# Seven products for eight in half of the Fourier columns of an in-projection, with the Fourier work and the rotation put behind them

## The chip, the cores and the metric

The kernel runs on one core of a Trainium2 chip. The metric is device time in microseconds (us), the median of the runs; lower is better. All arithmetic is in 32-bit floats. To keep float precision, the kernel writes each operand of a matrix product as a high part (`h`, the value rounded to the format that TensorE takes) and a low part (`l`, what the rounding left), and forms high·high + low·high + high·low: three matmuls where one would do.

## The reference, cut to what matters

```python
def hybrid_layer(x, ln_mix_g, w_in, w_fourier, attn_sink, ...):
    h = rmsnorm(x, ln_mix_g)
    z = h @ w_in                      # 2048 -> 2560 columns: 1024 Fourier, 1024 q, 256 k, 256 v
    zf, q, k, v = ...                 # split by columns
    of = fourier_mix(zf, w_fourier)   # 8 groups of 128 channels: Re(2-D DFT), then a 128x128 map
    q, k = apply_rope(q, cos, sin), apply_rope(k, cos, sin)
    oa = window_attention(q, k, v, attn_sink)
    mixed = concatenate([rmsnorm(of, g_of), rmsnorm(oa, g_oa)], axis=-1)
    x = x + mixed @ w_out
    u = relu(rmsnorm(x, ln_mlp_g) @ w_up)
    return x + (u * u) @ w_down
```

It is applied to 512 tokens of a prompt and 256 tokens of a sample, 768 in all (`T`). `HALF` is 384 tokens.

## The kernel before, in words

The kernel has five stages: a prologue (norm of x, transposes to `hh`, `hl`, and the v columns), the in-projection for all other columns, attention together with the output projection, the up-projection and the down-projection. The up-projection already uses seven products for eight. The change touches the in-projection alone, with the work that is laid beside it.

**The in-projection** takes the columns in units of 256: four units of the Fourier group, one of k, four of q (`cols`). A unit is four pieces, one for each quarter of the depth of 2048. A piece is one load of 512 KB (`piece_load`, tile `raw`), one split of the weights into `wh` and `wl` (ScalarE copies, VectorE subtracts), and 48 matmuls: two blocks of 128 columns, four depth blocks of 128, the three products of high and low parts, two halves of the tokens. After the fourth piece VectorE takes the four PSUM banks `pz` off as `zs`, scaled by `rb`, and a DMA writes them to DRAM (`zf`, `zk`, `zq`). There are 36 pieces, numbered from 0, and then attention.

**Other work is hung on pieces** by the table `todo`. `after(p, fn)` puts a function behind piece `p` or, for half numbers, in the middle of the next piece. Its matmuls then stand at this place in TensorE's own order, which is written out by hand. The other engines' orders are made by a scheduler, with the order of the code as priority. Only in the last four pieces are ScalarE and VectorE also in the order of the code. A DMA is issued by SyncE (loads), ScalarE (most stores) or GpSimd (a few stores); each of these issues in order, so a load that has to wait holds up every load behind it.

Three kinds of work hang there. First the eight Fourier groups (`load_group`, `fold`, `stage1`, `stage2`), one group for each two pieces, from piece 4.5 to piece 21.5. Then `fourier_norm` and `open_attention`, which loads the rotary tables. Then 16 rotation jobs, from piece 23 to 34.5: four `keys` and twelve `queries`. Each job loads half of the tokens of 128 rows back from DRAM into `rx`, and the rows with halves exchanged into `ry` by four small loads; GpSimd multiplies `ry` by the sines, VectorE multiplies `rx` by the cosines and adds; a query job then splits the result into a high tile `rh` and a low tile `rl` and stores both (`qh`, `ql`). `rx` and `ry` have two buffers each, `rh` and `rl` one. At piece 34.5 `load_of` loads the Fourier output of the first 128 tokens in two halves, `ofr`, into `ry` buffers; the output projection needs it as attention begins.

Of the kernel before, what the change touches and what calls it, by code (L numbers as in the profile page):

```python
# [20 lines left out]
P = 128  # L21
# [19 lines left out]
def hybrid_encoder(ctx: ExitStack, tc: tile.TileContext, a: dict):  # L41
# [3 lines left out]
    def f32(ap):  # L45
        return ap.bitcast(F32)
# [67 lines left out]

    zf_d = [dpool.tile([P, T], F32, tag=f"zf{i}", name=f"zf{i}") for i in range(FG)]
# [79 lines left out]
    with ExitStack() as ph:  # L195
# [142 lines left out]
        fp = fctx.enter_context(tc.tile_pool(name="fp", bufs=1, reuse_waits="tile"))  # L338
        cc = fp.tile([P, 2, P], F32, tag="cc", name="cc")
        nc.sync.dma_start(cc[:], a["c_chan"])  # L340
        tabh = fp.tile([P, 4, 256], F32R, tag="tabh", name="tabh")
        tabl = fp.tile([P, 4, 256], F32R, tag="tabl", name="tabl")
        for i in range(2):
            tab = fp.tile([P, 2, 256], F32, tag="zf", name="tab", bufs=2)
            nc.sync.dma_start(tab[:], a["c_pos"][:, 2 * i : 2 * i + 2, :])
            split(tabh[:, 2 * i : 2 * i + 2, :], tabl[:, 2 * i : 2 * i + 2, :], tab[:])
        ssf = fp.tile([P, T], F32, tag="ssf", name="ssf")
# [92 lines left out]
        kt = {}  # L440

        def open_attention():
            kp = kt["kp"] = kctx.enter_context(tc.tile_pool(name="kp", bufs=1, side="right", reuse_waits="tile"))
            for name, shape, src in (
                ("mask", [P, 384], a["c_mask"]), ("cosr", [P, T], a["c_cos"]), ("sinr", [P, T], a["c_sin"]),
# [3 lines left out]
                nc.sync.dma_start(kt[name][:, : src.shape[1]], src)  # L449
            kt["kdh"] = kp.tile([P, NKV, T], F32R, tag="kdh", name="kdh")  # L450
# [12 lines left out]
        def rows2(src, s):  # L463

            t0 = slice(s * HALF, (s + 1) * HALF)
            x, y = (kt["kp"].tile([P, 1, 512], F32, tag=c, name=c, bufs=n)[:, :, :HALF] for c, n in (("rx", 2), ("ry", 2)))
# [6 lines left out]
            return x[:, 0, :], t0  # L473

        def keys(i, s):
            x, t0 = rows2(zk_d[i], s)
# [21 lines left out]
        def load_q(u):  # L498
# [9 lines left out]
            y = kt["kp"].tile([P, 4, P], F32, tag="ry", name="ry", bufs=2)  # L508
# [21 lines left out]
        todo = {}  # L530

# [3 lines left out]
        for g in range(FG):  # L535
            p0 = 5.5 + 2 * g
# [1052 lines left out]
```

## Time and profile before

| | us |
|---|---|
| median of 3 runs (lowest, highest) | 2610.72 (2610.60, 2612.91) |
| the profiled execution, its span | 2610.32, 2608.5 |
| prologue, until the first matmul of the in-projection that runs on without a break | 0 to 56.7 |
| in-projection with the work beside it | 56.7 to 396.8 |
| attention and output projection | 396.8 to 752.4 |
| up-projection | 752.4 to 1686.2 |
| down-projection and the end | 1686.2 to 2608.5 |

The profile is of one execution. PE is TensorE, PEld its weight loads, DVE VectorE, ACT ScalarE, POOL GpSimd, SP SyncE; a "q" behind an engine's name is the DMA issuing of that engine. A group row gives line, engine, operation, tiles, shape and count, then busy us and mean ns of one, then the idle time before and what ended it. A chain row gives start, duration and what ran. A DMA row gives the size of one transfer and its median us from issue to landing.

### The profile page before, as it was taken

How to read it: one execution, taken by the hardware profiler on the slowest of the kernel's cores; microseconds unless marked ns; L12 is line 12 of the kernel's file. 1: busy time of each engine (PE TensorE's matmuls, PEld its weight loads, DVE VectorE, ACT ScalarE, POOL GpSimd, SP SyncE). 2: the span in 40 equal slices, each digit the busy share in tenths (PEclk: the TensorE clock that was granted, in tenths of full speed). 3: DMA queues.
4: the chain of work that ended last, by engine and by line, in shares of the span. 5: the costliest groups of instructions: out<-in, count | busy, mean ns of one | idle time of the engine just before them, and what ended most of it. 6: DMA issues, size and time to landing. Idle time of an engine off the chain costs nothing.

```text
span 2608.5 us, 35166 instructions
## 1 busy us (share of the span) xinstructions
PE 2595.5 (100%) x13692; PEld 2378.2 (91%) x13692; DVE 1739.1 (67%) x2186; ACT 1075.8 (41%) x1543; POOL 246.7 (9%) x347
## 2 busy tenths in 40 slices
PE   9999999999999999999999999999999999999998
PEld 9999998888899999999999999988888888888887
DVE  6334448777655656555777787757776765777687
ACT  6233327775323333333454445433333333333335
POOL 1011212234210011000000000010000000000000
PEclk9999999999999999999999999999999999999999
DMA  5323466345674555466666666685543672554364
GB/s 183 117 94 111 134 217 190 114 126 169 199 228 150 173 171 172 148 205 242 206 215 214 221 232 217 216 325 178 182 158 111 210 248 74 177 186 157 97 208 157
DMA packets 255047, 465.17 MB, mean 178 GB/s; under 512 B 20080, under 2 KB 151712, under 8 KB 254240
## 3 DMA queue, kind: packets, MB, share of 16 engines
q1 hardware_dynamic: 189936, 305.01, 36.5%
q10 hardware_dynamic: 53120, 110.46, 11.1%
q0 software_dynamic: 11824, 47.46, 5.4%
q8 instruction: 107, 1.75, 0.3%
q14 instruction: 60, 0.49, 0.1%
HBM read 344.10 MB, written 118.75 MB: 177 GB/s over the span
## 4 chain that ended last, share of the span: by engine, by line
PE 98%; DVE 1%; DMA 1%; issue 0%; ACT 0%; POOL 0%; SPq 0%; DVEq 0%; POOLq 0%; ACTq 0%
PE pu L970 36%; PE pd L1405 35%; PE pz L592 11%; PE pm L824 9%; PE pv L235 1%; PE s L635 1%; PE t L692 1%; PE o L711 1%; PE pa L396 1%; PE pe L417 0%; PE ptx L134 0%; PE pt L134 0%; DMA raw<-in_w_in 0%; DVE wl L70 0%; PE pz L417 0%
## 5 line engine op out<-in xcount | busy, mean ns | idle before, releaser
L970 PE MATMUL pu<-xf,wh 128*128 128x384 f32 x3072 | 781.1, 335 | 0.0
L970 PEld LDWEIGHTS pu<-xf,wh 128*128 128x128 f32 x3072 | 554.2, 188 | 1.5 <-ACT o L988 1.3
L1405 PE MATMUL pd<-wl,sh 128*128 128x512 f32 x1332 | 518.5, 389 | 0.0
L1405 PE MATMUL pd<-wh,sh 128*128 128x512 f32 x1332 | 518.5, 389 | 0.0
L1405 PE MATMUL pd<-wh,sl 128*128 128x512 f32 x1332 | 518.3, 389 | 0.0
L970 PE MATMUL pu<-xf,wl 128*128 128x384 f32 x1536 | 514.0, 335 | 0.0
L1382 ACT ACTIVATE wh<-rd 128x1024 fp32r<-128x1024 f32 x200 | 202.3, 1054 | 522.3 <-PE pd L1405 425.0
L1392 DVE TENSOR_TENSOR wl<-rd,wh 128x1024 fp32r<-128x1024 f32 x200 | 236.1, 1222 | 226.2 <-ACT wh L1382 225.5
L950 ACT ACTIVATE wh<-ur 128x1024 fp32r<-128x1024 f32 x160 | 170.0, 1063 | 382.0 <-PE pu L970 210.0
L1405 PEld LDWEIGHTS pd<-wh,sh 128*128 128x128 f32 x1332 | 250.2, 188 | 51.7
L1405 PEld LDWEIGHTS pd<-wl,sh 128*128 128x128 f32 x1332 | 250.2, 188 | 51.7
L1405 PEld LDWEIGHTS pd<-wh,sl 128*128 128x128 f32 x1332 | 250.1, 188 | 51.7 <-DVE sl L1393 0.3
L970 PEld LDWEIGHTS pu<-xf,wl 128*128 128x128 f32 x1536 | 288.4, 188 | 0.0
L956 DVE TENSOR_TENSOR wl<-ur,wh 128x1024 fp32r<-128x1024 f32 x160 | 195.6, 1222 | 75.4 <-ACT wh L950 75.4
L991 DVE TENSOR_TENSOR o<-pu,o 128x768 f32<-128x768 f32 x160 | 153.0, 956 | 122.4 <-PE pu L970 114.9
L592 PE MATMUL pz<-hh,wh 128*128 128x384 f32 x576 | 147.3, 336 | 0.0
L592 PE MATMUL pz<-hh,wl 128*128 128x384 f32 x576 | 146.5, 335 | 0.0
L592 PE MATMUL pz<-hl,wh 128*128 128x384 f32 x576 | 146.3, 335 | 0.0
L1375 DVE TENSOR_TENSOR rd<-rd 128x1024 f32<-128x1024 f32 x112 | 131.8, 1219 | 0.0
L970 PE MATMUL pu<-xs,wh 128*128 128x384 f32 x512 | 130.0, 335 | 0.0
L950 ACT ACTIVATE wh<-sx 128x1024 fp32r<-128x1024 f32 x64 | 67.8, 1062 | 131.0 <-PE pu L970 102.8
L70 DVE TENSOR_TENSOR wl<-raw,wh 128x1024 fp32r<-128x1024 f32 x56 | 68.3, 1225 | 68.9 <-ACT wh L69 68.8
(247 smaller groups left out, 3723.4 us busy)
## 6 DMA issues: line engine op xcount, KB each, us to landing
rd<-in_w_down SPq DMA_DIRECT2D x176, 512.0 KB, 4.8
ur<-in_w_up SPq DMA_DIRECT2D x128, 512.0 KB, 3.9
sr<-sd SPq DMA_DIRECT2D x95, 384.0 KB, 5.0
pd<-o ACTq DMA_DIRECT2D x60, 384.0 KB, 2.3
o<-pd POOLq DMA_DIRECT2D x60, 384.0 KB, 5.9
sd<-sm ACTq DMA_DIRECT2D x60, 384.0 KB, 2.7
raw<-in_w_in SPq DMA_DIRECT2D x40, 512.0 KB, 3.5
raw<-in_w_out SPq DMA_DIRECT2D x32, 512.0 KB, 4.3
```

The costliest lines, as they stand in the source:

```text
L70: nc.vector.tensor_tensor(out=lo, in0=src, in1=f32(hi), op=ALU.subtract)
L235: nc.tensor.matmul(pv[:, :256], l[j][:, i, t0], wv[j][r][:, i, :], start=(n == 0 and i == 0), stop=(n == 11 and i == 3),)
L592: nc.tensor.matmul(ps[c][s][:, :HALF], w[:, i, cs], h[j][:, i, s * HALF : (s + 1) * HALF], start=first and n == 0, stop=stop and n == 2,)
L824: nc.tensor.matmul(ps, l(k), w[:, k % 2, :], start=(k == 0 and n == 0), stop=(k == 7 and n == 2))
L950: nc.scalar.activation(wh[:], raw[:], AF.Copy)
L956: nc.vector.tensor_tensor(out=wl[:], in0=raw[:], in1=f32(wh[:]), op=ALU.subtract)
L970: nc.tensor.matmul(ps[:, t, :HALF], w[:, i, t * P : (t + 1) * P], xb[:, o, i, :], start=(s == first_of[bank] and i == 0 and n == 0), stop= ...
L991: nc.vector.tensor_tensor(out=o, in0=src, in1=o, op=ALU.add)
L1375: add = lambda x, y, op: nc.vector.tensor_tensor(out=x[:], in0=x[:], in1=y[:], op=op)
L1382: nc.scalar.activation(wh[:], t[:], AF.Copy)
L1392: nc.vector.tensor_tensor(out=wl[:], in0=t[:], in1=f32(wh[:]), op=ALU.subtract)
L1405: nc.tensor.matmul(o, l[:, q, ts], w[:, ns], start=(j == j0 and (q, t) == (0, 0)), stop=(j == j1 and (q, t) == (1, 2)),)
```

## The change

The first two Fourier units (columns 0 to 511, pieces 0 to 7) stay as they are. The other two (columns 512 to 1023) are now one unit, `strassen()`. The depth is cut in two halves `h`, and each half is treated as a product of 2x2 blocks: 512 columns as two blocks, the tokens as two, and the 128-deep blocks of the half as even and odd ones. In place of eight block products there are seven, in the form with a11, s1, s2, s4, s3, a12, a22 on the weight side. A block product is 24 matmuls of the same 128x384 shape. Sums of weight blocks are made by VectorE when needed (`f_sum`), each factor is split as before (`f_split`), and the products are added up in PSUM banks X, Y, Z and in four tiles `fo_` in SBUF (`f_out`). The sums of the token side are made once, in pieces 0 to 7: `factor_sums` is called four times, each time making four sums from `hh` and `hl`, splitting each into `thl`, and storing it through GpSimd's queue to DRAM tiles `td`. `f_right` loads them back as `tf`, 1536 KB each, two buffers, on SyncE's queue.

```diff
+        def factor_sums(h, q):
+            ...
+            def put(i, t, x=None):
+                x = place() if x is None else x
+                split(x[:, 0], x[:, 1], t)
+                nc.gpsimd.dma_start(t_d[h][i][:, :, 2 * q : 2 * q + 2, :], f32(x[:]))
+            x0 = place()
+            f11, f12 = new("f", 2), new("f", 2)
+            tt(f11, hi(0, 0), lo(0, 0), ALU.add)
+            tt(f12, hi(0, 1), lo(0, 1), ALU.add)
+            t1, t3 = new("t", 3), new("t", 3)
+            tt(t1, f12, f11, ALU.subtract)
+            put(0, t1, x0)
+            ...
+        fsteps = (
+            ("a11", (0, 0), "X"), ("s1", 0, "Y"), ("s2", 2, "X"), ("s4", (1, 1), "Y"), ("s3", 1, "X"), ("a12", (1, 0), "Z"), ("a22", 3, "X"),
+        )
+        ...
+        def f_right(h, s):
+            ...
+            x = fb[h, s] = tp_["p"].tile([P, 2, 4, HALF], F32R, tag="tf", name="tf", bufs=2)
+            nc.sync.dma_start(f32(x[:]), t_d[h][fsteps[s][1]][:])
+        ...
+        def open_strassen():
+            tctx_.close()
+            ...
+            for x in ("a11", "a21", "a22"):
+                f_load(0, x)
+            f_right(0, 1)
+            f_right(0, 2)
+            f_load(0, "a12")
+        def strassen():
+            nxt = lambda h, s, d: divmod(7 * h + s + d, 7)
+            f_split(0, 0)
+            f_sum(0, 1)
+            f_split(0, 1)
+            f_sum(0, 2)
+            for h in range(2):
+                for s in range(7):
+                    f_product(h, s)
+                    f_split(*nxt(h, s, 2))
+                    f_sum(*nxt(h, s, 3))
+                    if (h, s) != (0, 0):
+                        f_out(*nxt(h, s, -1))
+                    ...
+        for n, p in enumerate((0.25, 1.75, 3.25, 4.75)):
+            after(p, lambda n=n: factor_sums(n // 2, n % 2))
+        after(NP - 1.5, open_strassen)
...
+            if piece == NP:
+                strassen()
+                fctx_.close()
+                open_fourier()
+                piece_split(piece)
```

The rest of the columns follow as pieces 8 to 27: k, then q. Everything else that hung on pieces now hangs on these 20, with `NP` = 8. The Fourier groups come one for each piece instead of one for two, the rotation jobs about two for each piece. Quarter keys are new: work is also put a quarter into each half of a piece.

```diff
         for g in range(FG):
-            p0 = 5.5 + 2 * g
+            p0 = NP + 0.25 + 1 * g
             after(p0 - 1, lambda g=g: load_group(g))
             after(p0, lambda g=g: fold(g))
             for b in range(3):
-                after(p0 + 1 + b // 2 * 0.5, lambda g=g, b=b: stage1(g, b))
+                after(p0 + (1,1.25,1.5)[b], lambda g=g, b=b: stage1(g, b))
             after(p0 + 2, lambda g=g: stage2(g))
-        after(22.5, fourier_norm)
-        after(23, open_attention)
+        after(NP + 10, fourier_norm)
+        after(NP + 10.5, open_attention)
...
-            after(23 + i // 2 if i < 4 else 25 + (i - 4) * 10 // 12 if i < 12 else 31.5 + (i - 12), fn)
+        at_ = (10.5, 11, 11.5, 12, 12.5, 13, 13, 13.5, 14, 14, 14.5, 15, 15.5, 16.5, 17.5, 18.5)
...
-        after(34.5, lambda: load_of(0, [kt["kp"].tile([P, 4, P], F32, tag="ry", name="ofr", bufs=2) for _ in range(2)]))
+        after(NP + 18.5, lambda: load_of(0, [f32(kt["kp"].tile([P, 4, P], F32R, tag="ry", name="ofr", bufs=2)[:]) for _ in range(2)]))
```

The rotation has a third pair of buffers (`rx3`, in the place of the mask of attention, which is loaded later, and `ry3`), and two buffers `rl`. There is no `rh` any more: the high part of a query is written into its `ry` buffer, and stored from there.

```diff
-            x, t0 = rows2(zq_d[g][rs], s)
-            hi = kt["kp"].tile([P, HALF], F32R, tag="rh", name="rh")
-            lo = kt["kp"].tile([P, HALF], F32, tag="rl", name="rl")
-            split(hi[:], lo[:], x, HD ** -0.5)
-            nc.scalar.dma_start(qr_d[g][0][rs, t0], f32(hi[:]))
+            x, hi, t0 = rows2(zq_d[g][rs], s)
+            lo = kt["rq"].tile([P, HALF], F32, tag="rl", name="rl", bufs=2)
+            split(hi, lo[:], x, HD ** -0.5)
+            nc.scalar.dma_start(qr_d[g][0][rs, t0], f32(hi))
```

Three places show what this does to the engines' orders. A number behind a name tells tiles of the same name apart.

The first is VectorE in the early pieces. Before, from the split of the third piece's weights on, to the first Fourier fold (`fe`, `fo`, `fs`):

```order
L70 TENSOR_TENSOR wl_1028<-raw_967,wh_1027 128x1024
L70 TENSOR_TENSOR wl_1082<-raw_977,wh_1081 128x1024
L70 TENSOR_TENSOR wl_1136<-raw_1031,wh_1135 128x1024
L70 TENSOR_TENSOR wl_1202<-raw_1085,wh_1201 128x1024
L70 TENSOR_TENSOR wl_1256<-raw_1139,wh_1255 128x1024
L605 TENSOR_TENSOR zs_1165<-pz_969,rb_288 128x384
L605 TENSOR_TENSOR zs_1165<-pz_970,rb_288 128x384
L605 TENSOR_TENSOR zs_1193<-pz_971,rb_288 128x384
L605 TENSOR_TENSOR zs_1193<-pz_972,rb_288 128x384
L70 TENSOR_TENSOR wl_1314<-raw_1205,wh_1313 128x1024
L369 TENSOR_TENSOR fe_1350<-zf_1287 128x255
L369 TENSOR_TENSOR fo_1351<-zf_1287 128x255
```

Now, from the same split on (`raw_959` is the third piece's load); `f`, `t` are sums of the token side, `thl` their high and low parts:

```order
L70 TENSOR_TENSOR wl_1023<-raw_959,wh_1022 128x1024
L70 TENSOR_TENSOR thl_1040<-t_1045,thl_1040 128x768
L606 TENSOR_TENSOR t_1046<-t_1046,hl0_289 128x768
L70 TENSOR_TENSOR wl_1107<-raw_972,wh_1106 128x1024
L70 TENSOR_TENSOR thl_1053<-t_1046,thl_1053 128x768
L606 TENSOR_TENSOR t_1057<-t_1046,f_1041 128x768
L606 TENSOR_TENSOR f_1149<-hh1_290,hl1_291 128x768
L606 TENSOR_TENSOR t_1063<-hh0_288,t_1057 128x768
L70 TENSOR_TENSOR thl_1059<-t_1057,thl_1059 128x768
L606 TENSOR_TENSOR t_1063<-t_1063,hl0_289 128x768
L606 TENSOR_TENSOR f_1150<-hh1_290,hl1_291 128x768
L70 TENSOR_TENSOR wl_1191<-raw_1026,wh_1190 128x1024
```

Where VectorE had weight splits and banks to take off, nine of these twelve rows are now sums or splits of the token side. The Fourier folds have gone from these pieces.

The second is VectorE where the new unit begins. `fr` is a load of a weight block, `s3` a sum, and `zs_1519`, `zs_1547` are what the eighth piece leaves; `wl_1552` and `wl_1558` are the splits of the first and second product's weights:

```order
L70 TENSOR_TENSOR thl_1406<-t_1403,thl_1406 128x768
L803 TENSOR_TENSOR zs_1519<-pz_1252,rb_296 128x384
L803 TENSOR_TENSOR zs_1519<-pz_1253,rb_296 128x384
L656 TENSOR_TENSOR s3_1506<-fr_1507,fr_1509 128x1024
L656 TENSOR_TENSOR fr_1509<-fr_1509,fr_1511 128x1024
L656 TENSOR_TENSOR fr_1507<-fr_1509,fr_1507 128x1024
L803 TENSOR_TENSOR zs_1547<-pz_1254,rb_296 128x384
L803 TENSOR_TENSOR zs_1547<-pz_1255,rb_296 128x384
L70 TENSOR_TENSOR wl_1558<-fr_1509,wh_1557 128x1024
L70 TENSOR_TENSOR wl_1589<-fr_1507,wh_1588 128x1024
L656 TENSOR_TENSOR fr_1507<-fr_1517,fr_1507 128x1024
L70 TENSOR_TENSOR wl_1620<-fr_1507,wh_1619 128x1024
```

The second product's split `wl_1558` stands behind the three sums of weight blocks and behind the last bank of piece 7. SyncE's loads for this unit stand in this order (`tf_1513` is the token side of the second product, `tf_1515` of the third):

```order
L650 DMA fr_1507<-in_w_in 128x4x256
L650 DMA fr_1517<-in_w_in 128x4x256
L650 DMA fr_1509<-in_w_in 128x4x256
L650 DMA fr_1511<-in_w_in 128x4x256
L682 DMA tf_1513<-td0_0_70 128x3072
L682 DMA tf_1515<-td0_2_72 128x3072
L650 DMA fr_1627<-in_w_in 128x4x256
L650 DMA fr_1661<-in_w_in 128x4x256
L682 DMA tf_1625<-td0_1_71 128x3072
L682 DMA tf_1659<-td0_3_73 128x3072
```

In place of piece loads there are now loads of 512 KB and 1536 KB in turn, and each `tf` reads a `td` tile that two calls of `factor_sums` have stored.

The third is SyncE at the end of the in-projection, from the last rotation loads on. Before:

```order
L471 DMA ry_4007<-zq2_82 32x384
L468 DMA rx_4006<-zq2_82 128x384
L185 DMA ofr_4022<-ofd_90 128x4x128
L79 DMA raw_3980<-in_w_out 128x2x512
L185 DMA ofr_4023<-ofd_90 128x4x128
L79 DMA raw_4030<-in_w_out 128x2x512
L185 DMA ofr_4081<-ofd_90 128x8x128
```

Now:

```order
L482 DMA rx_4166<-zq2_90 128x384
L484 DMA ry_4167<-zq2_90 32x384
L485 DMA ry_4167<-zq2_90 32x384
L79 DMA raw_4066<-in_w_out 128x2x512
L484 DMA ry_4167<-zq2_90 32x384
L485 DMA ry_4167<-zq2_90 32x384
L186 DMA ofr_4181<-ofd_98 128x4x128
L569 DMA mask_4185<-in_c_mask 128x384
L79 DMA raw_4140<-in_w_out 128x2x512
L186 DMA ofr_4182<-ofd_98 128x4x128
L79 DMA raw_4191<-in_w_out 128x2x512
L186 DMA ofr_4243<-ofd_98 128x8x128
```

In both the last rows rotated come from `zq2`, and `ofr` follows. The load of the mask has been put between the two halves of `ofr`, and the buffer that the second half takes is now one from which a `qh` store reads.

More of the change, by code (lines that the diff above doesn't have):

```diff
@@ new lines, in f_out @@
+        def f_out(h, s):
+            q, more, bank = fouts[s]
+            if s == 6:
+                more = 0
+            for t in range(2):
+                o, x = fo_[q][:, t, :], fps[h, bank][t][:, :HALF]
+                if not more and h == 0:
+                    nc.scalar.activation(o, x, AF.Copy)
+                else:
+                    nc.vector.tensor_tensor(out=o, in0=x, in1=o, op=ALU.add)
+            if h == 1 and (more or s == 6):
+                hs = slice(q % 2 * HALF, (q % 2 + 1) * HALF)
+                rbb = rb[:, hs].rearrange("p (o t) -> p o t", o=1).to_broadcast([P, 2, HALF])
+                nc.vector.tensor_tensor(out=fo_[q][:], in0=fo_[q][:], in1=rbb, op=ALU.mult)
+                for t in range(2):
+                    nc.scalar.dma_start(zf_d[4 + 2 * (q // 2) + t][:, hs], fo_[q][:, t, :])
@@ L595, in hybrid_encoder @@
                             )
+                    if i == 1:
+                        for fn in todo.pop(piece - 0.75 + 0.5 * c, ()):
+                            fn()
                 if c == 0:
@@ L612, in hybrid_encoder @@
         last.close()
+        rctx.close()
     out_ctx = ExitStack()
```

147 lines of the change are left out of this document (127 added, 20 removed).

## The prediction

> **What bounds the kernel now.** I read the page first, then the chain of waits through the in-projection, then the busy time of each engine in stretches of it. The page says that TensorE is busy all the time and that the chain that ended last is TensorE's own:
>
> ```profile
> PE 2595.5 (100%) x13692; PEld 2378.2 (91%) x13692; DVE 1739.1 (67%) x2186; ACT 1075.8 (41%) x1543; POOL 246.7 (9%) x347
> PE 98%; DVE 1%; DMA 1%; issue 0%; ACT 0%; POOL 0%; SPq 0%; DVEq 0%; POOLq 0%; ACTq 0%
> ```
>
> So a matmul that goes is time that goes, if nothing takes its place. The chain by pieces shows it for the in-projection, with a row of the up-projection below, where sums and seven products are already in use:
>
> ```profile
> 56.66 53.66 PE pz L592 x308
> 110.76 8.32 PE pz L592 x48
> 119.09 1.43 PE pa L396 x12
> 120.52 4.16 PE pz L592 x24
> ...
> 292.69 104.11 PE pz L592 x600
> 397.04 1.40 PE pm L824 x6
> 761.60 924.60 PE pu L970 x5328
> ```
>
> A piece of 48 matmuls takes 8.32 us, half a piece 4.16, each 173.4 ns. 5328 matmuls of the same shape on sums that were loaded from DRAM take 924.60 us, 173.5 ns each. The form of the operand costs nothing. What the other engines and the transfers have to spare is in the stretches (columns: length, busy us and count of PE, PEld, DVE, ACT, POOL, granted clock, DMA share, GB/s):
>
> ```profile
> 56.60:122.00 65.40, 65.35 (x383) 65.34 (x383) 23.13 (x41) 14.51 (x28) 0.00 (x0) 1.00 0.38 122
> 122.80:181.00 58.20, 58.20 (x367) 57.63 (x367) 23.36 (x55) 19.81 (x45) 8.09 (x5) 1.00 0.32 110
> 292.70:360.00 67.30, 67.30 (x389) 67.30 (x390) 40.21 (x63) 19.80 (x31) 15.05 (x13) 1.00 0.64 199
> 360.00:396.60 36.60, 36.60 (x213) 36.60 (x212) 17.04 (x24) 9.37 (x13) 5.41 (x5) 1.00 0.69 212
> 1710.00:1720.00 10.00, 10.00 (x46) 8.29 (x45) 3.67 (x4) 4.28 (x5) 4.30 (x8) 1.00 1.03 420
> ```
>
> VectorE is busy a third of the early pieces, and the transfers at 0.64 to 0.69 where the rotation runs. The last row, of the down-projection, is the transfers at their limit: 420 GB/s.
>
> **What goes.** Eight pieces, 8 x 48 = 384 matmuls, become 2 x 7 x 24 = 336. 48 x 173.4 ns = 8.3 us go. The Fourier matmuls and all after the in-projection are the same in number and shape: nothing.
>
> **What is added in pieces 0 to 7.** The durations:
>
> ```profile
> L991 DVE TENSOR_TENSOR o<-pu,o 128x768 f32<-128x768 f32 x4 | 3.8, 956 | 2.2 <-PE pu L970 2.2
> L70 DVE TENSOR_TENSOR sl<-fs,sh 128x768 fp32r<-128x768 f32 x8 | 7.6, 952 | 1.0 <-ACT sh L69 1.0
> L69 ACT ACTIVATE sh<-fs 128x768 fp32r<-128x768 f32 x8 | 6.6, 831 | 1.1 <-DVE fs L369 1.1
> L70 DVE TENSOR_TENSOR wl<-raw,wh 128x1024 fp32r<-128x1024 f32 x44 | 53.4, 1222 | 67.8 <-ACT wh L69 67.7
> L933 DVE TENSOR_TENSOR sx<-ur 128x1024 f32<-128x1024 f32 x2 | 2.4, 1222 | 1.4 <-DMA ur<-in_w_up 1.4
> L605 DVE TENSOR_TENSOR zs<-pz,rb 128x384 f32<-128x384 f32 x36 | 18.5, 552 | 32.1 <-PE pz L592 32.0
> ```
>
> Four calls with 8 sums and 4 splits each are 48 VectorE operations of 128x768 at some 0.95, 46 us; with seven `wl` (8.6) and four `zs` (2.2) that is 57 us of the 66.6 that pieces 0 to 7 last. ScalarE gets 16 x 0.83 = 13 us more. The weights are split up to three pieces ahead, so TensorE is not held there: nothing. But VectorE, free for two thirds before, ends only shortly before the unit begins at 56.7 + 66.6 = 123.3. The row after which the first weight block of the second product may be loaded (`thl_1393`, whose buffer lies where `fr_1509` goes) is fifth from the end of the sums: 58.1 + some 50 us of work, and 2 us that I allow for waits, 110.3.
>
> **The start of the unit.** `fr_1509` waits until GpSimd's store of that tile, 768 KB, has landed. SyncE issues in order, so `fr_1511`, `tf_1513` and `tf_1515` are queued behind it. Rows for the transfers (KB of one, median us to landing):
>
> ```profile
> zq<-zs POOLq DMA_DIRECT2D x2, 384.0 KB, 6.3
> sd<-sm POOLq DMA_DIRECT2D x2, 384.0 KB, 6.2
> sd<-o POOLq DMA_DIRECT2D x2, 384.0 KB, 5.1
> gf<-in_ln_final_g POOLq DMA_DIRECT2D x1, 1024.0 KB, 12.6
> raw<-in_w_in SPq DMA_DIRECT2D x40, 512.0 KB, 3.5
> xt<-in_x_prompt SPq DMA_DIRECT2D x2, 1024.0 KB, 5.5
> zf<-zs ACTq DMA_DIRECT2D x8, 384.0 KB, 2.3
> zq<-zs ACTq DMA_DIRECT2D x6, 384.0 KB, 4.0
> ```
>
> Call the landing of the store T0. Both weight blocks are there at T0 + 0.4 + 3.5; two sums (2.4), the last bank of piece 7 (1.1), the split `wl_1558` (1.2) and small gaps (0.6) make T0 + 9.2. The second product is wanted at 123.3 + 4.16 = 127.5. Its `tf_1513` follows 1 MB of `fr`: 2.6 MB at 420 GB/s and about 2 us are T0 + 8.2. So T0 may be 118.3. With half the bytes, stores on this queue took 5.1 to 6.3; the other half at 420 GB/s is 0.9 more, so 7.2 at least, and 12.6 at most, the row of 1024 KB. With the issue (0.6) T0 is 118.1 to 123.5, and the stall 0 to 5.2. I take 8.7, nearer to the rows of the same kind: T0 = 119.6, stall **1.3**.
>
> By the Trainium skill, page "DMA: Bandwidth & Descriptors", section on the anatomy of one DMA, a transfer on GpSimd's path takes 2.0 us and its bytes at 436 GB/s: an estimate of 2.9 us for 384 KB, where these rows show 5.1 to 6.3, and of 3.8 us for the 768 KB here, with which this stall would be nothing and the sum 1.3 us lower. The trace disagrees for stores on this queue, and for a load of 512 KB agrees (3.2 by the page, 3.5 in the row).
>
> **The rest of the unit.** Each product has a 1536 KB load or none, two of seven with only two steps (8.3 us) between the release of the buffer and the use. By 420 GB/s and 2 us it takes 5.8; by the 1024 KB row, stretched, 8.2. The unit moves 19 MB in 58 us (eight `fr`, eight `tf`, eight stores of 192 KB, two `raw`), 330 GB/s, below the 420. I take **0.3**, bounds 0 and 3. VectorE's sums, splits and take-offs are some 45 us of 58, in the order of need: nothing. Nor do I expect the first Fourier fold to be late: its loads come after the unit's end, with two pieces (16.6 us) and more until its matmuls; where it is late by a load, that is 3 us.
>
> **The rotation.** Twelve query jobs get three pairs of buffers instead of two, but `ry` is now held until the store of the high part has landed. In the trace before:
>
> ```profile
> qh<-rh ACTq DMA_DIRECT2D x12, 192.0 KB, 3.9
> ry<-zq SPq DMA_DIRECT2D x48, 48.0 KB, 2.5
> DMA to landing us min/median/max: 1.8/3.5/8.1
> L459 POOL TENSOR_TENSOR ry<-ry,sinr 128x384 f32<-128x384 f32 x16 | 18.3, 1146 | 74.8 <-DMA ry<-zq 44.3 <-DMA ry<-zk 14.3 <-DMA rx<-zq 8.9
> ACT rh L72 <- DMA qh<-rh: 8.1, 2, 5.4
> 388.53 0.36 SPq L185 DMA_DIRECT2D ofr<-ofd  x1
> 400.10 0.40 PE L824 MATMUL pm<-wh,ofh 128*128 128x512 f32 x1
> ```
>
> (The third row is the landing of `qh`, the fifth the waits of ScalarE for it, us, times, longest.) A buffer's cycle is four issues (1.8), landing (2.5), sines (1.15), add (0.6), split (0.5) and the store's landing L: 6.6 + L, and by three buffers a job each 2.2 + L/3. From key 12.5 to 15.5 nine jobs are hung on three pieces, 25 us, 2.8 us each. With L = 3.9 a job takes 3.5, and the nine end 6.3 us late; after them come jobs only each 8.3 us, so that this is made good. What is queued behind: on VectorE the split of piece 26's weights (`wl_3989`), which stands behind the thirteenth job; by my walk it has 0.7 us to spare at L = 3.9, and each us of L takes 9/3 = 3 us. On SyncE the second half of `ofr` (issued 388.53 before, 8.3 us ahead of the end of `pz`) and the weights behind it, which now wait for the last `qh` to land; TensorE wants this half at 400.10, 3.3 us after the end of `pz`, and a load of this kind and the split need over 6. By the walk that costs 0 at L = 3.5 and 3 to 4 at 4.6, of which the delay through `wl_3989` is a part.
>
> Which L? The same rotation goes from 97 us into about 67: 97 us at some 203 GB/s were 19.7 MB, less 12 pieces of weights of 0.52 MB 13.4 of its own; with 8 such pieces now that is 17.6 MB, 263 GB/s, by the rows above (0.64 at 199) a share of 0.85. The 384 KB stores took 2.3 us in the stretches at 0.32 and 4.0 in those at 0.64. So L rises above 3.9; a narrower flow holds itself back, so not to 5.4. I take 4.3: **2.4** for the tail, bounds 0 and 12 (L = 8.1).
>
> **The sum**, against the profiled execution's 2610.32: -8.3 + 1.3 + 0.3 + 2.4 = -4.3, **2606.0 us**. The median of the runs shown, 2610.72, is 0.4 higher, which I leave aside. A measurement of this kernel can tell about 0.2%, 5.2 us, from no change.
>
> **The rivals.**
>
> *All is covered.* T0 in time, L at 3.5 to 3.9: -8.3 to -6, 2602.0 to 2604.3. For it speak TensorE's unbroken chain before, and that loads by SyncE land in 3.5 us; against it the two waits on stores, which are new. The page named above speaks for this case at the unit's start.
>
> *The stores of the sums land slowly.* GpSimd's 768 KB need 12.6 us, four of them close together: the unit starts 5.2 us late, later `tf` loads 1 to 2: with the tail -8.3 + 5.2 + 1.5 + 2.4 = +0.8, 2611.1, within 0.2%. Against it: the queue's 384 KB rows at 5 to 6.
>
> *The rotation can't keep its pace.* `ry` is given back only when `qh` has landed; at a share of 0.85 the landings reach the longest that the trace shows, 8.1 us, and the job in which `wl_3989` is queued comes 3 x (8.1 - 4.1) = 12 us late for TensorE, and `ofr` and the weights of the output projection with it: -8.3 + 1.6 + 12 = +5.3, 2615.6, and some us more if attention's start is held as well. It is slower than before from L = 4.1 + 6.7/3 = 6.3 on. For it: the waits for `qh` in the trace (5.4 the longest), at a third less load. Against it: the median of 3.5 to 3.9.
>
> That the change doesn't do what it says can be left out: the matmuls are counted from the order.
>
> **How the numbers follow.** My forecast, 2604.3 to 2608.5, has 0.40 (of it 0.06 faster by over 0.2%, the rest within), all covered 0.31, slow stores 0.11 (within), the rotation's pace 0.18 (nearly all slower by over 0.2%, as the price goes up from there). Faster 0.37, within 0.45, slower 0.18. The range is 2602.0 to 2615.6: it holds the first three cases and the beginning of the fourth.
>
> **What would show it.** Right: seven-product matmuls at 173 ns, `pf` without a gap but for one of 1 to 2 us before the second product, released by VectorE's `wl`; a gap of 1 to 4 us at piece 26 or just after the last `pz`, with `qh` landing in 4 to 5 us; the up- and down-projection unchanged. Wrong: gaps in pieces 0 to 7 (VectorE too full), a wait of the Fourier's first matmuls, `qh` over 6 us, or more than 5 us between the first and the second product.

## The result, and the profile after

The changed kernel takes 2618.79 us (median of 9 runs, 2616.58 to 2620.16), the kernel before 2610.60 beside it (9 runs, 2610.18 to 2612.91): a ratio of 1.0028, interval 1.0018 to 1.0038. It is slower, by 8.2 us; 2606.0 was predicted, with 2615.6 as the upper end. (Of all runs below, one execution, of the kernel that stores `qh` and `ql` by GpSimd, took 4336.31 us at a granted clock of 0.556 and is left out.) The profiled execution took 2616.86, span 2615.1, which is 6.6 more than the span before.

The page first: engine times, the shares of the chain that ended last, and the queue that GpSimd issues to (packets, MB, share).

```profile
PE 2589.7 (99%) x13644; PEld 2370.5 (91%) x13644; DVE 1808.5 (69%) x2264; ACT 1098.6 (42%) x1573; POOL 257.8 (10%) x363
PE 94%; DMA 2%; DVE 2%; issue 0%; POOL 0%; ACT 0%; SPq 0%; POOLq 0%; DVEq 0%; ACTq 0%
q0 software_dynamic: 14128, 60.04, 6.5%
```

TensorE has 48 matmuls less (13692 before) and is busy 5.8 us less, but it is no longer 98% of the chain. The chain through the unit of seven products:

```profile
57.07 66.17 PE pz L787 x380
123.23 8.33 PE pf L697 x48
131.58 8.71 DMA tf<-td
140.43 41.84 PE pf L697 x240
182.27 10.40 PE pz L787 x60
```

The unit lasts 182.27 - 123.23 = 59.04 us; its 336 matmuls at 173.4 ns are 58.25, so it lost 0.8. (The 8.71 of `tf` is no stall of that length: the chain goes back along the transfer that ended the one short wait of the unit, 0.6 us below, while TensorE worked beside it.) What TensorE waited for from 50 to 460 us (us in total, times, longest):

```profile
PE pz L787 <- ACT wh L69: 8.5, 1, 8.5
PE pm L1025 <- DVE ofl L70: 1.0, 1, 1.0
PE pm L1023 <- DVE wl L70: 0.6, 1, 0.6
PE pf L697 <- DMA tf<-td: 0.6, 1, 0.6
PE pm L1023 <- ACT ofh L69: 0.5, 1, 0.5
```

One wait stands out: 8.5 us before piece 26, for the split of its weights. The stretches show the first pieces, the gap, and what follows (length, busy us and count of PE, PEld, DVE, ACT, POOL, granted clock, DMA share, GB/s):

```profile
56.00:122.00 66.00, 65.95 (x381) 65.64 (x381) 57.59 (x66) 21.88 (x26) 11.18 (x16) 1.00 0.82 306
378.00:380.00 2.00, 0.00 (x0) 0.00 (x0) 1.02 (x2) 0.52 (x1) 0.36 (x1) 0.50 0.83 269
383.00:384.00 1.00, 1.00 (x4) 1.00 (x4) 0.84 (x2) 0.03 (x1) 0.00 (x0) 0.50 0.39 111
385.00:386.00 1.00, 1.00 (x7) 1.00 (x6) 0.08 (x1) 0.46 (x1) 0.00 (x0) 1.00 0.94 355
```

In the gap the granted clock falls to 0.50, and it stays there for 2.9 us after the matmuls begin again: 4 of them fall wholly or partly into a microsecond, 7 at full clock. 2.9 us at half rate cost 1.5 us more.

The last place is the program's end. SyncE's last store, of the kernel after and then of the kernel before:

```profile
2608.86 0.42 SPq L1525 DMA_DIRECT2D out_y_sample<-acc  x1
```

```profile
2604.13 0.41 SPq L1326 DMA_DIRECT2D out_y_sample<-acc  x1
```

From this issue to the end of the span it is 2615.1 - 2608.86 = 6.2 us after, 2608.5 - 2604.13 = 4.4 before.

| | us |
|---|---|
| eight products become seven | -8.3 |
| the unit's stalls; start of the pieces (57.07 for 56.66) | +0.8, +0.4 |
| gap before piece 26, and the half clock behind it | +8.5, +1.5 |
| attention (357.1 for 355.4: `ofh`, `ofl`, `wl` above) | +1.7 |
| program end | +1.8 |
| sum (measured: +6.6) | +6.4 |

So the seven products brought what they should. The rotation took it back and more.

### Why the gap is there

GpSimd's sine products mark the rotation's pace (start, us, and the idle time before with what ended it):

```profile
337.24 1.19 POOL L467 TENSOR_TENSOR ry<-ry,sinr 128x384 f32<-128x384 f32 x1 [4.72 <-DMA ry<-zq]
...
377.37 0.99 POOL L467 TENSOR_TENSOR ry<-ry,sinr 128x384 f32<-128x384 f32 x1 [3.41 <-DMA ry<-zq]
```

Eight jobs in 40.1 us: 5.0 each, where 2.8 was planned and 3.6 predicted (2.2 + 4.3/3). Behind the last of these stands the split for piece 26, in ScalarE's timeline:

```profile
374.58 0.52 ACT L72 ACTIVATE ry<-rx 128x384 fp32r<-128x384 f32 x1 [5.02 <-DMA qh<-ry]
...
378.98 0.52 ACT L72 ACTIVATE ry<-rx 128x384 fp32r<-128x384 f32 x1 [3.88 <-DVE rx L469]
...
380.50 1.06 ACT L69 ACTIVATE wh<-raw 128x1024 fp32r<-128x1024 f32 x1 [0.99 <-DVE rl L73]
```

The landing of `qh` isn't the reason: it is below the 4.3 us that I took.

```profile
DMA to landing us min/median/max: 1.9/3.3/6.1
```

The reason is in SyncE's timeline, where the four small loads of one `ry` stand behind one another:

```profile
357.66 0.43 SPq L79 DMA_DIRECT2D raw<-in_w_in  x1
...
361.02 0.90 SPq L484 DMA_DIRECT2D ry<-zq  x1
364.12 0.30 SPq L485 DMA_DIRECT2D ry<-zq  x1
...
372.85 0.30 SPq L484 DMA_DIRECT2D ry<-zq  x1
375.20 0.30 SPq L485 DMA_DIRECT2D ry<-zq  x1
```

The fourth load at 364.12 has the same source and the same buffer as the third at 361.02, and yet it comes 2.2 us after the third's issue had ended. In the chain of waits it follows `357.66 6.44 DMA raw<-in_w_in`, a load of weights with which it has nothing to do. The fourth at 375.20 follows `369.59 5.59 DMA qh<-ry`, the store of another job. The program's own rows show how. The waits of one job's loads and of one store, as built (each `DMAHW` is a counter of finished transfers; there are eight, 0 to 7):

```
L482 DMA rx<-zq_88 128x384 [waits DMAHW2_49,DVE_49,Activation_49]
L484 DMA ry<-zq_88 32x384 [waits DMAHW3_49,Pool_49]
L485 DMA ry<-zq_88 32x384 [waits DMAHW4_49]
L484 DMA ry<-zq_88 32x384 [waits DMAHW5_49]
L485 DMA ry<-zq_88 32x384 [waits DMAHW6_49]
...
L505 DMA qh_92<-ry 128x384 [waits DMAHW7_49,Activation_49]
```

Only the first load of `ry` needs the buffer's release. Each of the others waits for a counter all the same: the transfers of SyncE and ScalarE take these eight in turn, and one can't be issued until the one that had its counter last has landed. A query job has seven transfers, so a job and a weight load are once round. Any slow transfer stops SyncE at the next that has its counter, and in SyncE's order everything behind it. SyncE's waits between 312 and 400 us have these rows for them, among others:

```profile
SPq L485 <- DMA qh<-ry: 5.6, 2, 3.5
SPq L485 <- DMA raw<-in_w_in: 2.2, 1, 2.2
SPq L484 <- DMA ry<-zq: 2.2, 2, 1.5
```

Between the two rows of GpSimd above, in 40 us, SyncE issued 46 transfers at some 0.4 us each, which is 20 us. The waits that ended at a load's own counter add up to some 15 us, and those for a buffer to some 5, of which 2.8 are one wait for an `rx` that a key job still held. Three of the counter waits, before the loads at 351.51, 364.12 and 375.20, are 3.6, 2.2 and 2.0 us long, 7.8 together, against a gap of 8.5. So in this kernel the waits for counters are seen, and the chain that ends in the gap goes through them.

### The profile page after: what moved, and what is told of

The parts are those of the page before. It is cut to its first block, busy times and chain, and to the rows that moved or that the text cites. A ratio compares the mean times of both kernels' runs of the same rounds, so it can differ in the third digit from the quotient of the medians.

```text
span 2615.1 us, 35297 instructions
## 1 busy us (share of the span) xinstructions
PE 2589.7 (99%) x13644; PEld 2370.5 (91%) x13644; DVE 1808.5 (69%) x2264; ACT 1098.6 (42%) x1573; POOL 257.8 (10%) x363
## 3 DMA queue, kind: packets, MB, share of 16 engines
q0 software_dynamic: 14128, 60.04, 6.5%
## 4 chain that ended last, share of the span: by engine, by line
PE 94%; DMA 2%; DVE 2%; issue 0%; POOL 0%; ACT 0%; SPq 0%; POOLq 0%; DVEq 0%; ACTq 0%
PE pu L1169 36%; PE pd L1604 35%; PE pm L1023 9%; PE pz L787 6%; PE pf L697 2%; PE pv L236 1%; PE o L910 1%; PE t L891 1%; PE s L834 1%; PE pa L402 1%; DMA raw<-in_w_in 1%; DMA ry<-zq 0%; PE pe L423 0%; PE ptx L135 0%; DVE kdl L497 0%
## 5 line engine op out<-in xcount | busy, mean ns | idle before, releaser
L787 PE MATMUL pz<-hh,wh 128*128 128x384 f32 x448 | 115.7, 339 | 8.5 <-ACT wh L69 8.5
L787 PE MATMUL pz<-hh,wl 128*128 128x384 f32 x448 | 114.3, 336 | 0.0
L787 PE MATMUL pz<-hl,wh 128*128 128x384 f32 x448 | 114.2, 336 | 0.0
L1592 DVE TENSOR_TENSOR sl<-sr,sh 128x768 fp32r<-128x768 f32 x111 | 105.6, 951 | 0.0
```

What stands on the lines that cost most here:

```text
L787: nc.tensor.matmul(ps[c][s][:, :HALF], w[:, i, cs], h[j][:, i, s * HALF : (s + 1) * HALF], start=first and n == 0, stop=stop and n == 2,)
L1592: nc.vector.tensor_tensor(out=sl[:], in0=sr[:], in1=f32(sh[:]), op=ALU.subtract)
```

## The experiments

Three theories stood against each other. **Counters**: the pace is set by the number of transfers, through waits as above. **Buffer**: it is set by `ry` being held until its store lands, as in the prediction. **Order**: ScalarE and VectorE have the splits of weights behind too many jobs (up to six between two splits). Ratios are to the kernel before, run beside each kernel. Jobs are counted from the first key job; jobs 5 to 13 are the eight intervals measured above.

**One `ry` load for four.**

```diff
-            for r in range(0, P, 64):
-                nc.sync.dma_start(y[r : r + 32], z[r + 32 : r + 64])
-                nc.sync.dma_start(y[r + 32 : r + 64], z[r : r + 32])
+            nc.sync.dma_start(y, z)
```

> The four loads of ry in each rotation job become one load of the same 192 KB, in which the two 32-row halves are not exchanged (this part of the rotation is left out, all operations on the engines stay). Theory 'counters': a transfer is issued only when the one before it on the same completion counter has landed; eight counters serve the loads of SyncE and the stores of ScalarE, and a query job takes seven of them, so a job can't begin before stores and weight loads of the job before have landed. Then four transfers per job for seven bring the pace of the query jobs from 5.0 us to about 3.5, the gap before piece 26 falls from 8.5 to 0 to 2 us, and the time to 2604 to 2609. Theory 'store' (that of the prediction): ry is held until qh has landed; buffers and landing are the same, so pace and gap stay and the time is 2617 to 2620. Theory 'traffic': the same bytes, 2616 to 2620.

2612.83 (2611.23 to 2614.22), ratio 1.0004 [0.9994, 1.0013]: 6.0 us below the changed kernel, less than the counters promised (2604 to 2609), and jobs 5 to 13 still took 5.1 us each, not 3.5. Its one large wait is of another kind:

```profile
PE pz L785 <- DVE zs L801: 5.1, 1, 5.1
```

The scheduler had put the take-off of a PSUM bank behind rotation jobs. The order counts, too.

**Three `ry` loads** (the two middle blocks of 32 rows in one strided transfer).

```diff
+            nc.sync.dma_start(y[0:32], z[32:64])
+            nc.sync.dma_start(y[96:128], z[64:96])
+            nc.sync.dma_start(y[32:96], z.rearrange("(b p) o t -> b p o t", p=32)[0:4:3])
```

> The four loads of ry become three, with the exchange: the two middle blocks of 32 rows come in one transfer. Nothing is left out. Counters: six transfers per query job for seven, pace 5.0 to about 4.4, the gap 8.5 to 3 to 5 us, 2611 to 2615. Store and traffic: no change, 2617 to 2620.

2626.58, 1.0051 [1.0036, 1.0066]: 7.8 us slower than with four, against the counters' number.

```profile
PE pz L787 <- DVE zs L803: 6.3, 2, 4.4
PE pz L787 <- ACT wh L69: 4.6, 1, 4.6
```

Again bank take-offs that the scheduler laid behind jobs. A small edit changes its order everywhere, so this run decides nothing between the theories, and the first is uncertain for the same reason.

**The stores `qh` and `ql` by GpSimd**, which leaves the eight counters to the loads.

```diff
-            nc.scalar.dma_start(qr_d[g][0][rs, t0], f32(hi))
-            nc.scalar.dma_start(qr_d[g][1][rs, t0], lo[:])
+            nc.gpsimd.dma_start(qr_d[g][0][rs, t0], f32(hi))
+            nc.gpsimd.dma_start(qr_d[g][1][rs, t0], lo[:])
```

> qh and ql are stored by GpSimd's queue, which has counters of its own, and not by ScalarE. Counters: five transfers per query job on the eight shared counters, none of them a store: pace about 4, gap 0 to 4, 2606 to 2614. Store: on this queue 384 KB took 5.1 to 6.3 us before, so ry is held longer: the gap grows and the time is 2619 to 2624.

2617.78, 1.0021 [1.0011, 1.0031], between what the two theories expected. The waits and the queue's row:

```profile
PE pz L787 <- ACT wh L69: 3.2, 1, 3.2
PE pm L1023 <- ACT ofh L69: 2.6, 1, 2.6
```

```profile
q0 software_dynamic: 15664, 64.76, 7.0%
```

From job 6 to 12 a job took 3.9 us, 5.4 in the changed kernel; from job 5 to 13 it is 4.5 for 5.0. Over these eight jobs SyncE's waits for counters fell from 15 to 2.7 us, while those for a buffer held by `qh` rose to 8.5; the gap shrank from 8.5 to 3.2. The time hardly moved, because the program's end grew with the packets (to 8.2 us from the last store, +2.0) and attention's start waited longer for `ofh`.

**The packing behind, without the seven products**: 16 ordinary Fourier pieces, and all else as after.

```diff
-        NP = 8
+        NP = 16
-        after(NP - 1.5, open_strassen)
+        after(NP - 1.5, tctx_.close)
```

> Only the schedule is changed, not the products: the four Fourier units are 16 ordinary pieces, no sums are made, and the Fourier work and the rotation are hung on the 20 pieces behind them exactly as in the changed kernel. If the packing of the rotation is the whole loss, the gap of 8 to 9 us with its half clock and the handoff are there as in the changed kernel: 2618.8 + 8.3 - 0.8 = 2626 (2624 to 2628). If the new unit is a part of it (transfers or buffers that it leaves late), the gap is smaller and the time is 2612 to 2620.

2626.47, 1.0052 [1.0037, 1.0067], as expected, with a gap of 6.8 us: the packing alone makes the kernel before 15 us slower, and the products take 8 of them off.

```profile
PE pz L780 <- ACT wh L69: 6.8, 1, 6.8
```

**ScalarE and VectorE in code order four pieces earlier**, so that no split stands behind six jobs.

```diff
-            if piece == n_in - 4:
+            if piece == n_in - 8:
```

> ScalarE and VectorE work in the order of the code for the last eight pieces, not the last four; nothing else changes. In the changed kernel six rotation jobs stand between two weight splits on these engines; now three at most. Theory 'order and pace' (a weight split stands behind jobs, and jobs come at 5.0 us each because their transfers wait for completion counters): the pace stays near 5, the gap before piece 26 shrinks from 8.5 to 0 to 5, but sixteen jobs still end late, so that 2 to 5 us come back at the start of attention: 2611 to 2617. Theory 'pace alone' (the end is set by the last job wherever the splits stand): 2616 to 2620.

2617.91 (2616.51 to 2619.72), 1.0022 [1.0013, 1.0032]. The long wait becomes several (4.2 in all for `wh`, 1.7 for `wl`), but the end of the rotation is as late. That is the time of "pace alone"; order alone is worth under 1 us. It gives a base, though, on which the number of transfers can be changed with the order kept: next **one `ry` load on it** (four transfers a job, and the halves not exchanged).

```diff
-            if piece == n_in - 4:
+            if piece == n_in - 8:
...
+            nc.sync.dma_start(y, z)
```

> As e9_code_order, with one load of ry for four, rows not exchanged (that part of the rotation is left out): four transfers per query job for seven, with ScalarE's and VectorE's work in the same order over the last eight pieces. Order and pace, with the counters as its cause: pace 3.5 to 4, gap 0 to 2, 2603 to 2609, at least 5 below e9_code_order. If the pace is that of buffers held by stores, or of the engines' own work: within 2 us of e9_code_order.

2614.23, 1.0009 [1.0000, 1.0019]: 3.7 less, which lies between the two expectations (at least 5, and at most 2). And **one transfer more, with the same bytes**: `rx` in two loads on the same base.

```diff
-            nc.sync.dma_start(x, z)
+            nc.sync.dma_start(x[0:64], z[0:64])
+            nc.sync.dma_start(x[64:128], z[64:128])
```

> As e9_code_order, with rx loaded in two transfers of 64 rows for one of 128: eight transfers per query job for seven, same bytes, same order of ScalarE's and VectorE's work in the last eight pieces. Counters: a job's pace rises from 5.0 by a seventh, 0.6 to 0.8 us, some 8 us over twelve jobs, 2621 to 2627 against 2617.9 of e9_code_order. If only bytes, buffers held by stores, or the engines' work set the pace: 2616 to 2620.

2625.09, 1.0052 [1.0037, 1.0067]: 7.2 more, the time that the counters gave.

```profile
PE pz L788 <- ACT wh L69: 6.7, 3, 3.2
PE pm L1024 <- ACT ofh L69: 3.1, 1, 3.1
```

Four, seven and eight transfers a job give 2614.2, 2617.9 and 2625.1 with the order of the code kept: the time goes with their number, though not in a straight line. Over all twelve query jobs the pace goes with it too: 4.4, 5.2 and 5.7 us each. But over jobs 5 to 13, those ahead of the split that was late, it was 5.0, 4.9 and 5.3, and the traces don't show that the difference goes through the counters. Sorted by the built program's waits, SyncE waited for a load's own counter 0, 4.9 and 5.7 us over these jobs, not 15 as in the changed kernel. The eighth transfer added 0.8 us of such waits and 6.3 us of issuing (52 transfers in 24.0 us for 44 in 17.7), so what an in-order queue needs to issue it is a rival that these runs don't part from the counters. What SyncE waits for instead, with seven transfers and then with four (312 to 400 us):

```profile
SPq L482 <- DMA zq<-zs: 5.2, 1, 5.2
SPq L482 <- DMA qh<-ry: 4.0, 1, 4.0
```

```profile
SPq L483 <- DMA qh<-ry: 11.1, 7, 3.3
SPq L482 <- DMA zq<-zs: 5.6, 1, 5.6
```

The wait for `zq` is that of the thirteenth job. It is the first of the third query group, and its own rows come from the unit that ends with piece 23; they have yet to be taken off and stored. All runs with the order of the code and sixteen jobs have this wait, of 5.2 to 8.3 us; in the changed kernel the rows had landed (367.0) before their load was issued (369.4). With four transfers the largest sum of waits over jobs 5 to 13 is for a `ry` held until `qh` has landed (10.2 us), the reason that the prediction had named: where the counters let go, the buffer and the source take over.

**Five transfers, by merging both stores** (and three `ry` loads; high and low part side by side in one 384 KB store).

```diff
-            nc.scalar.dma_start(qr_d[g][0][rs, t0], f32(hi))
-            nc.scalar.dma_start(qr_d[g][1][rs, t0], lo[:])
+            nc.scalar.dma_start(qr_d[g][rs, :, t0], f32(hl_))
```

> As e9_code_order, with five transfers per query job for seven and nothing left out: ry in three loads, and high and low part side by side in the ry buffer, stored by one transfer of 384 KB. Counters: pace 4 to 4.5, gap 0 to 3, 2605 to 2611, between the other two. Store: ry is held longer, by a larger store that waits for the low part too: slower than e9_code_order by 1 to 4 us.

2630.15, 1.0071 [1.0056, 1.0086], the slowest of all, and 12 us above its base, where the buffer theory had 1 to 4. The merged store holds twice the buffer and waits for the low part too: a `ry` load issued at 350.82 had waited 1.1 us for the store issued at 347.13. But such waits are only some 3 us of SyncE's in jobs 5 to 13; 8.4 are for an `rx` that the split of the low part still reads, and 8.3 for the thirteenth job's rows. The sign is that of the buffer theory; which of these makes the 12 us isn't shown.

```profile
PE pz L786 <- ACT wh L69: 9.4, 4, 5.3
```

**GpSimd stores and code order together.**

```diff
-            if piece == n_in - 4:
+            if piece == n_in - 8:
...
+            nc.gpsimd.dma_start(qr_d[g][0][rs, t0], f32(hi))
+            nc.gpsimd.dma_start(qr_d[g][1][rs, t0], lo[:])
```

> Both single edits together, sixteen jobs, nothing left out: qh and ql through GpSimd's queue, so that loads don't wait for the counters of stores, and ScalarE and VectorE in the order of the code for eight pieces, so that a weight split stands behind three jobs at most. Order and pace: pace about 3.9 as in e3, last job some 5 us earlier than in e9, gap 0 to 2, 2606 to 2613. If a store's landing on this queue or ry held by it sets the pace, no better than either alone: 2616 to 2620.

2621.84, 1.0040 [1.0027, 1.0054]: worse than either edit alone, a miss. The thirteenth job came at 379 us, after a wait of 6.1 us for `zq`, and in the chain the load of `ofr` follows the last `qh`. Jobs 5 to 13 took 5.3 us each, though SyncE waited only 1.6 us for counters. The profiled span is 3.1 us above that of the order of the code alone; 2.0 of it are the program's end, which grows with GpSimd's packets as above, and 1.0 is a wait in the unit of seven products. So the two edits didn't add up: the stores cost at the end, and the thirteenth job was held by its source.

**Twelve jobs for sixteen**: the third query group is rotated in attention, as the fourth is already.

```diff
-            if g < NKV - 1:
+            if g < NKV - 2:
-            if g == NKV - 1:
+            if g >= NKV - 2:
-        at_ = (10.5, 11, 11.5, 12, 12.5, 13, 13, 13.5, 14, 14, 14.5, 15, 15.5, 16.5, 17.5, 18.5)
+        at_ = (10.5, 11, 11.5, 12, 12.5, 13, 13.5, 14, 14.5, 15, 15.5, 16.5)
```

> The four jobs of the third query group are gone from the in-projection; its queries are rotated in attention as those of the fourth group already are. Twelve jobs at 5 us fit into the 75 us of pieces 19 to 27: order and pace expects the gap before piece 26 and the half clock gone, and 2603 to 2608, if attention has VectorE time for six more rotations of 64x512 (VectorE is busy 165 of 208 us there); if not, attention gives back 3 to 10 us. If the loss came from something else in this stage, the gap stays: 2614 or more.

2612.20 (2610.61 to 2614.83), 1.0001 [0.9991, 1.0010]. The gap is gone:

```profile
PE pz L787 <- DVE zs L803: 0.9, 2, 0.5
```

The last `pz` ends at 389.9, some 7 us earlier than in the kernel before. But attention then takes 361 us for 355.4. **The sine products of both groups in attention by GpSimd** instead of VectorE:

```diff
-                rotate(state[u]["x"][:HD], state[u].pop("y")[:HD], slice(b * P, (b + 1) * P), nc.vector)
+                rotate(state[u]["x"][:HD], state[u].pop("y")[:HD], slice(b * P, (b + 1) * P), nc.gpsimd)
```

> As e5_twelve_jobs, but in attention the products with the sines are made by GpSimd (busy 61 of 208 us there) and not by VectorE (165). In e5 the last pz ended 7 us earlier than before the change and attention took 5.6 us longer. If that is VectorE's added work (a quarter of it goes to GpSimd: 12 operations of 64x512, some 8 us), attention gives back 0 to 3 us and the time is 2605 to 2610, faster than both kernels. If attention takes longer for another reason (queries that come later through GpSimd, or its own loads), 2611 to 2615.

2610.72 (2609.36 to 2611.62), 0.9996 [0.9987, 1.0005], attention 359.4, so it gives back 4 us and not 0 to 3: level with the kernel before, the best version found. **The same move in the kernel before** shows what the products are then worth:

```diff
-            if g < NKV - 1:
+            if g < NKV - 2:
...
+                rotate(state[u]["x"][:HD], state[u].pop("y")[:HD], slice(b * P, (b + 1) * P), nc.gpsimd)
```

> The kernel before, with the one edit of e13: the third group's queries are rotated in attention (GpSimd multiplies by the sines), twelve jobs in the in-projection. It says what this edit costs without the new unit. In e13 attention took 359.2 us (last pz to first pu) against 355.4 before. If the edit itself costs these 4 us: in-projection as before, 2614 to 2617. If attention in e13 is longer because it begins with less done ahead of it: 2610 to 2612.

2615.33, 1.0015 [1.0005, 1.0024]: the move costs some 4 us by itself, and with it the seven products, with their packing, bring 2615.3 - 2610.7 = 4.6, with the longer program end already paid.

**The sums stored by ScalarE instead of GpSimd**, first in the changed kernel, then in the version with twelve jobs.

```diff
-                nc.gpsimd.dma_start(t_d[h][i][:, :, 2 * q : 2 * q + 2, :], f32(x[:]))
+                nc.scalar.dma_start(t_d[h][i][:, :, 2 * q : 2 * q + 2, :], f32(x[:]))
```

> The changed kernel with the one edit that the sixteen stores of the token sums are issued by ScalarE. The order of the rotation on ScalarE and VectorE is the same. Queue theory: tail 8.3 for 10.1, and the gap before piece 26 stays (8 to 9 us with half clock behind it): 2616 to 2618. Otherwise 2618 to 2620.

> As e13_twelve_jobs_pool, but the sixteen stores of the token sums are issued by ScalarE and not through GpSimd's queue. From the last matmul to the end of the span it is 8.2 us in the kernel before and 8.3 in e6_schedule_alone (11824 packets on GpSimd's queue), 10.1 in all kernels with the sums stored through it (14128), 12.0 in the two that store the queries through it too (15664). Theory 'the queue's transfers cost time at the program's end': the tail falls from 10.1 to 8.3 and the time from 2610.7 to 2608 to 2609.5, below the kernel before. If the tail belongs to something else in the new unit (its number of transfers or of waits), it stays at 10.1 and the time at 2610 to 2612. ScalarE and the eight shared counters get sixteen transfers more in pieces 0 to 7: 0 to 2 us at the unit's start.

2620.31, 1.0033 [1.0021, 1.0044], and 2613.00 (2610.54 to 2614.91), 1.0004 [0.9995, 1.0013]. In both the program end is back at 4.6 to 4.7 us, as the queue theory said, but neither time is in the range that it gave: the unit of seven products is some 4 to 5 us longer, since TensorE now waits there for ScalarE's splits and falls to the half clock. Queue and waits of the first of the two:

```profile
q0 software_dynamic: 11824, 47.46, 5.4%
```

```profile
PE pz L787 <- ACT wh L69: 8.4, 1, 8.4
PE pf L697 <- ACT wh L69: 1.5, 1, 1.5
```

## Why the prediction was wrong, step by step

**The products: right.** -8.3, at 173 ns, and the form of the operand cost nothing.

**Pieces 0 to 7: right.** VectorE was busy 57.6 us of 66 (57 predicted), and TensorE didn't wait. VectorE was done sooner than taken, though: its last split of a sum ended at 111.9 us, 11 before the unit began.

**The unit's start: the stall didn't come.** 1.3 us were predicted before the second product, and there is none. The 0.8 us that the unit lost are mostly a wait of 0.6 for a later `tf` load, where 0.3 was taken; a `tf` load came at 8.3, as stretched. Two terms put T0, the landing of the store, too late. The store was issued at 107.6 us, not at 110.9, and it landed in 4.2, not 8.7: T0 was 111.8, not 119.6, where 118.3 would have done. With either term right T0 comes out at 116.3 or 115.1, and no stall is predicted.

```profile
td<-thl POOLq DMA_DIRECT2D x16, 768.0 KB, 4.5
```

4.5 us, where I took 8.7 from rows of 384 KB at 5 to 6. (The lower bound of 7.2 went from the slowest of those rows; from the fastest, 5.1, it is 6.0.) Here the estimate of 3.8 from the Trainium skill's page "DMA: Bandwidth & Descriptors" was nearer than mine, which had read the queue's slow rows as its price.

**The Fourier folds: right.** None was late.

**The rotation: this is the step that failed**, and in it the pace, "a job each 2.2 + L/3". The place was right (the weights of piece 26, behind the thirteenth job, then `ofr`), and so was the sign. L was even lower than taken (3.3, with the transfers' share at 0.78 from 345 to 392 us and not 0.85), and by the formula the gap should have been nothing; it was 8.5 us. The formula has one resource, the buffer, and lets the loads be issued as soon as it is free. But SyncE issues in order, and each load waits for the counter of a transfer of something else. The buffers gave a pace of 3.3 by L = 3.3; it was 5.0, with 15 us of 40 spent waiting for counters. This much the trace and the built program show for the changed kernel. The experiments show that the rotation's packing makes the loss: without the seven products it is there as well, and with twelve jobs the gap is gone. That the counters alone set the pace they don't show. Where the waits for them were nearly gone, with one `ry` load, the twelve query jobs took 4.4 us each for 5.2, but jobs 5 to 13 still took 5.0 to 5.1: waits for buffers, that held by `qh` foremost, and for the job's own rows, for which the formula has no term either, had taken their place. The rival on the pace had the right end (slower, from a late split), by a cause that wasn't there: landings up to 8.1 us.

**Left out altogether**: the half clock behind the gap (1.5 us) and the longer program end (1.8).

**Open.** How much of the gap would go with the counters' waits alone isn't shown, since every edit that took them away changed something else too. The changed kernel's runs scatter over 3.6 us and its profiled execution lies 1.9 below its median; where those 1.9 us go isn't shown. Nor are the 4 us that the move to attention costs broken down. No version here is faster than the kernel before by more than the runs can tell.

## What to carry to other kernels

When work is packed tighter, count the transfers of each step and not only its bytes and buffers: in a program whose queues share a few completion counters, each load waits for the landing of the one that had its counter, whatever that was. Look in the built program for a wait that the data doesn't need, and price a step's pace by issue, counters, buffers and the arrival of its source together: with one of them gone, the next took over here. A stall that is long enough (here 2.6 us or more) is paid again in clock, and a transfer put on another queue can be paid at the program's end.

## What the runs showed of the hardware

**The clock after a stall.** In the changed kernel the granted clock was 0.50 from 377.72 us for 6.83 us, 4.6 us after TensorE had gone idle. Over the runs such spells lasted 3.41, 6.83 or 10.24 us (the last with the ordinary Fourier pieces), one to three times 3.41. The Trainium skill, page "TensorE: Matmul & The Clock Gate", section "Part 1: The HAM clock gate", has half rate after an idle window of some 3.4 us and full rate after a busy one of the same length; the lengths of the spells agree. The idle time doesn't: with the stores of `qh` and `ql` by GpSimd a spell began after a wait of 2.6 us, and with the sums stored by ScalarE one at 130.25 us after waits of 1.5 and 0.7 us close together. In the sixteen profiles, between 60 and 2600 us, a spell came with every wait of a matmul of 2.6 us or more, and the longest wait with no spell near it was 1.7 us. In the changed kernel full rate came back after 2.9 us of matmuls.

**The program's end.** From SyncE's last store to the end of the span it took 4.4 to 4.7 us in the five profiles with 11824 packets on GpSimd's queue, 6.2 in the nine with 14128, and 8.2 in the two with 15664. The order is always the same, and moving the 16 stores of sums off that queue took the time back. It isn't proportional: the first 2304 packets more cost 1.5 to 1.8, the next 1536 another 2.0. By transfers it is 16 and then 24 more, and neither row shows why.
